# Moving the keys and values of a memory from behind the experts into an earlier mixer, and gathering expert rows without scale and bias

## The chip, the cores and the metric

One core of one Trainium2 chip runs the whole program in one launch. The metric is the device time of one execution in microseconds (us), lower is better; several executions give a median. TensorE (PE) multiplies matrices, VectorE (DVE) and ScalarE (ACT) work element by element, GpSimd (POOL) and SyncE (SP) here mostly issue DMA transfers. Weights lie in HBM and are brought to SBUF by DMA; matmuls accumulate in PSUM.

## The reference, cut to what matters

Two transformer blocks follow one another on 256 tokens of 1024 channels, all in float32.

```python
for l in range(2):                                   # first block
    mix = hybrid_mixer(x, ...)                       # delta rule, convolution branch, forgetting attention
    x = layer_norm(ALPHA * x + mix, ln_mix_g[l], ln_mix_b[l])
    ff = swiglu(x, ...) if l == 0 else moe_swiglu(x, ...)     # top 2 of 8 experts of width 3584
    x = layer_norm(ALPHA * x + ff, ln_ffn_g[l], ln_ffn_b[l])
# second block
x = x + 0.5 * swiglu_ffn(rms_norm(x, ffn1_norm), ...)
mem_kv = rms_norm(mem, mem_norm) @ w_mem_kv          # memory: 256 tokens, depends on inputs alone
m_k, m_v = split(mem_kv); m_k = rms_norm(m_k per head, m_k_gain)
...                                                  # second mixer: attention, state space, memory attention
x = x + 0.5 * swiglu_ffn(rms_norm(x, ffn2_norm), ...)
return rms_norm(x, final_norm)
```

The memory's keys and values need nothing of the first block; they are read only in the second block's mixer.

## The kernel before, in words

**Arithmetic.** A float32 product is made of three matmuls in a faster format: each operand is split into a high and a low part (hi x hi, hi x lo, lo x hi; `mm3`, L183 to L185). A weight tile is loaded by SP (`load`, L166) into one of a ring of places, 1 MB each, and `part` splits each half of it: ScalarE copies it to `wh` (L172), VectorE subtracts to get `wl` (L174). `proj_a` and `proj_b` are projections of 48 matmuls each (256 columns) into a PSUM bank with the tag `a`.

**Order.** The stages stand one behind the other in `build`: mixer 0, ffn0, mixer 1, MoE, ffn1, mixer 2, ffn2, final norm. Within a stage the code emits pieces, and the framework's list scheduler sets the order on each engine's queue; what is emitted earlier has precedence. `issue_after` holds operations of one engine behind a named one. The places of the load ring are a list (`self.places`): 4 `raw` tiles normally; in the MoE also `early0` to `early4`, the tile `rows`, and the two operands `xTh` and `xTl`.

**Mixer 1** emits the delta rule's inverse, its scan, the forgetting attention, the convolution branch (which holds one of the two PSUM banks `a` from its first matmul until L765) and last the gates (L787: one `proj_b` of 48 matmuls, a copy L790, a sigmoid, a product L792). Behind these the parts of the mixed output are transposed and split, the convolution's part last (L802, L803), and the output projection runs.

**MoE.** `layer_norm_T` normalises the rows (L852), transposes them, applies scale and bias on the transposed copy (L859, L860), and then also applies scale and bias to the rows themselves: four operations of 128x1024 on VectorE (L867). The router's logits (L907), the choice of two experts, and the position of each token in its expert's list (`pos`, L921 to L925) follow. The rows are split to `xtokh` and `xtokl` (L930, L931). `gather` brings the rows of an expert into 128 slots by matmuls with a 0/1 matrix (L994), 8 matmuls a step and 4 steps an expert; the high part goes to `xeh` (L996, ScalarE), the low part to `xel` (L998, VectorE). Four experts have 128 slots, and the other four stand in two pairs with 64 each, whose high and low gathers are added into one `xef` (L1000). The loop then runs 42 steps of up projection, activation and down projection; `combine` adds weighted results to the accumulator `acc` (L1062 to L1070), which starts as ALPHA times the rows (L1113, one operation).

**End of the MoE.** Before the last combine, `memory_load` fetches the memory's normalised transposed rows (`memd`, written to DRAM in ffn0) and the weights `mem_k` and `mem_v`, and splits three of their four halves. The statistics of the next layer norm (L1146) and seven small operations that count tokens beyond an expert's slots (L1150 to L1156) follow. An `If` (L1159) holds a path for such tokens, which is not taken here. Behind it come the layer norm (L873 to L879), `rms_T` (squares L1234, scaling L1239, transposes L267), `memory_keys` (2 x 48 matmuls, a head norm with L1263, L1265 and L1267, a copy, a store) and then ffn1.

Of the kernel before, what the change touches and what calls it, by code (L numbers as in the profile page):

```python
# [28 lines left out]
NE = 8  # L29
# [74 lines left out]
class Net:  # L104
# [249 lines left out]
    def mixer1(self, l, x, xT):  # L354
# [443 lines left out]
        self.emit(inverse(), scan(), fox(), conv(), gates())  # L798
# [43 lines left out]
    def layer_norm_T(self, tp, tag, r, st, rows, name, n=4, z_="lnz", bufs=4):  # L842
# [58 lines left out]
    def moe(self, fp, x, xT):  # L901
# [23 lines left out]
        V.tensor_scalar(pos, pos, -1.0, None, op0=ALU.add)  # L925

# [50 lines left out]
        def gather(u, g):  # L977
# [11 lines left out]
            for k in range(0, 8, 2):  # L989
                pg = self.ps("t", "gat").rearrange("p (a k n) -> p a k n", a=2, k=2)  # L990
                for j in range(2):
                    for a, src in enumerate((xh, xl)):
                        for t in range(2):
                            PE.matmul(pg[:, a, j, :], src[:, t, (k + j) * P:(k + j) * P + P], o[:, t],  # L994
                                      start=t + a + j == 0, stop=t == 1, skip_group_check=True)
                S.activation(g[0][:, k:k + 2, :], pg[:, 0], AF.Copy)  # L996
                if len(u) == 1:
                    self.last = V.tensor_copy(g[1][:, k:k + 2, :], pg[:, 1])  # L998
                else:
                    self.last = V.tensor_tensor(g[0][:, k:k + 2, :], g[0][:, k:k + 2, :], pg[:, 1], op=ALU.add)  # L1000
                if k == 6 and u != (0,):
                    back[u] = places(u)
                yield
# [54 lines left out]
        def combine(py, ohT, gp):  # L1058
# [5 lines left out]
            for t in range(2):  # L1064
                for h in range(2):
# [4 lines left out]
                    V.tensor_tensor(acc[:, t, hs], acc[:, t, hs], pc, op=ALU.add)  # L1070

# [40 lines left out]
        with self.tc.issue_after(self.last.ins):  # L1112
            V.tensor_scalar(acc, x, ALPHA, None, op0=ALU.mult)  # L1113
# [27 lines left out]
        st = self.new_stats()  # L1141

        def stats():
            for t in range(2):
                for h in range(2):
                    V.bn_stats(out=st[:, t, h, :], in_=acc[:, t, h * 512:h * 512 + 512])  # L1146


        cap, mxf, mxi = fp.tile([P, NE], F32, name="cap"), fp.tile([P, 1], F32, name="mxf"), fp.tile([P, 1], I32, name="mxi")
        V.tensor_scalar(cap, rank, 3.5, 64.0, op0=ALU.is_lt, op1=ALU.mult)  # L1150
        V.tensor_scalar(cap, cap, 64.0, None, op0=ALU.add)
        V.tensor_tensor(pos, pos, cap[:, None, :].to_broadcast([P, 2, NE]), op=ALU.subtract)
        V.tensor_tensor(cap, cnt, cap, op=ALU.subtract)
        V.tensor_reduce(mxf, cap, axis=AX.X, op=ALU.max)
        V.tensor_scalar(mxf, mxf, 0.0, None, op0=ALU.max)
        V.tensor_copy(mxi, mxf)  # L1156
        most = nc.values_load(mxi[0:1, 0:1], min_val=0, max_val=T)
        stats()
        with self.tc.If(most > 0):  # L1159
            ecur = fp.tile([P, 1], F32, name="ecur")  # L1160
            V.memset(ecur, 0.0)
            with self.tc.For_i(0, NE, 1) as e:
# [18 lines left out]
                for k in range(8):  # L1181
# [4 lines left out]
                    V.tensor_copy(x2[:, k, :], pg[:, :P])  # L1186
# [37 lines left out]
                stats()  # L1224
        return acc, st, mem
# [31 lines left out]
    def norm_heads(self, tp, ps, n, gain, out, tag="g", sq="nhsq"):  # L1257
# [4 lines left out]
        sq = tp.tile([P, 512], F32, name=sq, bufs=2)  # L1262
# [69 lines left out]
    def memory_load(self, fp, tags):  # L1332

        mT = [fp.tile([P, 8, T], F32R, name="memT", tag=t) for t in tags]
        for i in range(2):
            self.nc.gpsimd.dma_start(mT[i], self.memd[i])
        raw = [self.load(self.A[n]) for n in ("mem_k", "mem_v")]
        return mT, raw, [self.part(raw[0]), self.part(raw[0], 1024), self.part(raw[1])]

    def memory_keys(self, fp, mT, raw, parts):  # L1340

        kept = self.keep_mem(fp, tag="y")
        ps = self.proj_a(None, mT, parts=parts[:2])
        self.table(SILU, self.norm_heads(fp, ps, 2, self.col2("mkg"), self.mkT.rearrange("p c t -> p (c t)"), "y", "mos"))
        ps = self.proj_b(None, mT, parts=[parts[2], self.part(raw[1], 1024)])
        self.nc.scalar.activation(self.mv, ps, AF.Copy)
        self.memk = self.dp.tile([P, 1024], F32, name="memk")
        self.nc.gpsimd.dma_start(self.memk, kept)
# [499 lines left out]
def build(tc, A, out):  # L1848
    with ExitStack() as ctx:
# [18 lines left out]
        with net.banks(a=2, y=4, t=2), pool("moe") as fp:  # L1868
            rows = net.load_rows(fp.tile([P, 2, D], F32, name="rows"), "ln_mix", 2, 2)
            xT = net.layer_norm_T(fp, "t", r, st, rows, "mix1", z_="mos", bufs=2)  # L1870
            r, st, mem = net.moe(fp, r, xT)
# [3 lines left out]
            net.memory_keys(fp, *mem)  # L1875
# [28 lines left out]
```

## Time and profile before

| | us |
|---|---|
| median of 3 runs | 2171.85 |
| lowest and highest | 2169.86, 2173.09 |
| profiled execution | 2181.34 |
| its span in the trace | 2179.6 |
| TensorE busy in it | 2085.4 |
| VectorE busy | 1301.9 |
| ScalarE busy | 1021.4 |

The durations in the trace belong to the profiled execution, and sums are made against its time. The span runs from the first to the last instruction; the rest of the execution's time lies around it. A busy TensorE is not a TensorE at its peak: the clock that it was granted is given apart, as a share of full speed (1.00 is 2.4 GHz, 0.50 is 1.2 GHz).

### The profile page before, as it was taken

The page shows a single profiled execution, that of the slowest core. Times are in us where ns is not written, and L with a number is a line of the kernel's source. Part 1 is how long each engine was busy: PE and PEld are TensorE (multiplying, and loading weights), DVE is VectorE, ACT ScalarE, POOL GpSimd, SP SyncE. Part 2 cuts the span into 40 slices and gives each one's busy share as a digit, 9 for nine tenths or more (in the row PEclk, how much of TensorE's full clock was granted, in tenths as well). Part 3 has the DMA queues.
Part 4 walks back from the last instruction along what each step waited for, and adds up shares of the span by engine and source line. Part 5 has one row for each costly group of instructions (what it writes and reads, how often), then busy time and mean ns, then how long its engine had stood idle before and what let it go on. Part 6 is the DMA issues. An engine that isn't in the chain of part 4 may idle for free. (4 is left out here: it accounts for less than half of the span.)

```text
span 2179.6 us, 31865 instructions
## 1 busy us (share of the span) xinstructions
PE 2085.4 (96%) x12770; PEld 1606.4 (74%) x12770; DVE 1301.9 (60%) x1911; ACT 1021.4 (47%) x1453; POOL 13.0 (1%) x27
## 2 busy tenths in 40 slices
PE   8998999899979999999999999999799999999998
PEld 7887999788766565566565566554799988888997
DVE  6767954766676555555465455443655568665544
ACT  6545444464545444444354345442544444544443
POOL 0000000000000000000000000000000000000000
PEclk9979999998979999999999999999899999999999
DMA  6313675322359999999999999998455553444552
GB/s 236 103 44 117 213 261 179 136 88 98 140 181 348 363 407 381 412 419 376 404 367 396 387 404 406 417 415 352 171 188 191 187 176 125 136 164 155 184 183 97
DMA packets 78987, 545.37 MB, mean 250 GB/s; under 512 B 8960, under 2 KB 11272, under 8 KB 13936
## 3 DMA queue, kind: packets, MB, share of 16 engines
q1 hardware_dynamic: 76112, 527.40, 63.4%
q0 software_dynamic: 2720, 15.86, 2.0%
q8 instruction: 103, 1.69, 0.3%
q14 instruction: 52, 0.43, 0.1%
HBM read 536.74 MB, written 6.49 MB: 249 GB/s over the span
## 5 line engine op out<-in xcount | busy, mean ns | idle before, releaser
L174 DVE TENSOR_TENSOR wl<-raw,wh 128x1024 fp32r<-128x1024 f32 (+1 forms) x662 | 798.1, 1217 | 436.4 <-ACT wh L172 422.4
L172 ACT ACTIVATE wh<-raw 128x1024 fp32r<-128x1024 f32 (+1 forms) x662 | 690.6, 1054 | 629.0 <-PE a_pA L184 276.1
L183 PE MATMUL a_pA<-xTh,wh 128*128 128x256 f32 x1456 | 421.0, 290 | 5.9 <-ACT foxqk L620 3.3
L185 PE MATMUL a_pA<-xTh,wl 128*128 128x256 f32 x1456 | 417.9, 287 | 0.9 <-DVE wl L174 0.9
L184 PE MATMUL a_pA<-xTl,wh 128*128 128x256 f32 x1456 | 418.2, 287 | 0.0
L183 PEld LDWEIGHTS a_pA<-xTh,wh 128*128 128x128 f32 x1456 | 283.4, 195 | 13.7 <-ACT foxqk L620 5.3
L184 PEld LDWEIGHTS a_pA<-xTl,wh 128*128 128x128 f32 x1456 | 283.5, 195 | 4.8 <-issue 3.4
L185 PEld LDWEIGHTS a_pA<-xTh,wl 128*128 128x128 f32 x1456 | 283.3, 195 | 4.2 <-issue 2.7
L1021 PE MATMUL a_up<-raw,xef 128*64 128x512 f32 x896 | 213.5, 596 | 0.0
L184 PE MATMUL a_up<-wl,xeh 128*128 128x512 f32 x448 | 180.7, 403 | 0.5 <-DVE wl L174 0.4
L183 PE MATMUL a_up<-wh,xeh 128*128 128x512 f32 x448 | 177.3, 399 | 0.0
L185 PE MATMUL a_up<-wh,xel 128*128 128x512 f32 x448 | 177.1, 395 | 0.0
L1021 PEld LDWEIGHTS a_up<-raw,xef 128*64 128x64 f32 x896 | 65.2, 137 | 127.7 <-issue 122.6
L183 PE MATMUL a_pB<-wh,xTh 128*128 128x256 f32 x480 | 142.0, 297 | 5.0 <-ACT glu L620 3.1
L1026 DVE TENSOR_TENSOR mos<-mos,a_up 128x512 f32<-128x512 f32 x42 | 28.7, 684 | 192.2 <-PE a_up L1021 141.5
L184 PE MATMUL a_pB<-wl,xTh 128*128 128x256 f32 x480 | 140.4, 293 | 0.0
L185 PE MATMUL a_pB<-wh,xTl 128*128 128x256 f32 x480 | 139.4, 293 | 0.6 <-DVE xTl L278 0.6
L1054 PE MATMUL y_y<-raw,mof 128*64 128x512 f32 x448 | 132.8, 602 | 0.7 <-ACT mof L1040 0.7
L184 PEld LDWEIGHTS a_up<-wl,xeh 128*128 128x128 f32 x448 | 84.6, 189 | 35.1 <-issue 12.2
L183 PEld LDWEIGHTS a_up<-wh,xeh 128*128 128x128 f32 x448 | 84.6, 189 | 27.5 <-ACT wh L172 7.3
L185 PE MATMUL acc_acc<-wh,ffl 128*128 128x512 f32 x264 | 102.0, 392 | 0.0
L184 PE MATMUL acc_acc<-wl,ffh 128*128 128x512 f32 x264 | 101.9, 392 | 0.0
(558 smaller groups left out, 2717.9 us busy)
## 6 DMA issues: line engine op xcount, KB each, us to landing
raw<-in_moe_w_dram SPq DMA_DIRECT2D x336, 1024.0 KB, 9.3
raw<-in_ffn_in_dram SPq DMA_DIRECT2D x44, 1024.0 KB, 4.8
raw<-in_ffn_w_dram SPq DMA_DIRECT2D x33, 1024.0 KB, 4.9
raw<-in_w_in_a_dram SPq DMA_DIRECT2D x24, 1024.0 KB, 5.0
raw<-in_ffn_out_dram SPq DMA_DIRECT2D x22, 1024.0 KB, 4.8
raw<-in_w_out_dram SPq DMA_DIRECT2D x12, 1024.0 KB, 4.9
raw<-in_w_in_g_dram SPq DMA_DIRECT2D x12, 1024.0 KB, 4.9
raw<-in_w_in_b_dram SPq DMA_DIRECT2D x6, 1024.0 KB, 5.0
```

What stands on the lines that cost most here:

```text
L172: nc.scalar.activation(wh[:, :m], raw[:, o:o + m], AF.Copy)
L174: nc.vector.tensor_tensor(wl[:, :m], raw[:, o:o + m], wh[:, :m].bitcast(F32), op=ALU.subtract)
L183: mm(out, lh, rh, start=start, stop=False, skip_group_check=True)
L184: mm(out, lh, rl, start=False, stop=False, skip_group_check=True)
L185: mm(out, ll, rh, start=False, stop=stop, skip_group_check=True)
L1021: PE.matmul(ps[r], xe[0][:, k0, r], w[:, k * 512:k * 512 + 512], start=k0 == 0, stop=k0 == 7, skip_group_check=True)
L1026: V.tensor_tensor(s, s, pp[1], op=ALU.mult)
L1054: PE.matmul(py[h][r], hf[:, k, r], w[:, j * 1024 + h * 512:j * 1024 + h * 512 + 512], start=b == 0 and k == 0, stop=b == 6 and k == 3, ski ...
```

## The change

1. Memory's keys and values are computed in mixer 1, emitted between the convolution branch and the gates. The transposed rows of the memory come by two POOL loads into two of the four `raw` tiles; the weights come through the ordinary load ring. Keys and values are stored in two halves from tiles with the tag `sg`. `memory_load` and the call behind `rms_T` go.
2. In the MoE `layer_norm_T` no longer applies scale and bias to the rows. The gather sums the high and low gathers in one PSUM region; two ScalarE activations of 128x128 per step then apply scale and bias (a scalar per partition, from `gain` and `shift`). For a 128-slot expert another copy and a subtraction split the result again. The accumulator is made by four operations of 128x1024 that apply ALPHA, scale and bias, and that read `rows`. The path under the `If` applies scale and bias as well.
3. The count of tokens beyond the slots is emitted at step 4 of the loop instead of behind it; its value is still read at the end.
4. The statistics are emitted one by one behind each of the last adds.

```diff
@@ mixer1
-        self.emit(inverse(), scan(), fox(), conv(), gates())
+        self.emit(inverse(), scan(), fox(), conv(), *([self.memory_keys(mp)] if l else []), gates())
@@ layer_norm_T
-        with self.tc.issue_after(last.ins):
-            for t in range(2):
-                for i, op in enumerate((ALU.mult, ALU.add)):
-                    V.tensor_tensor(r[:, t, :], r[:, t, :], rows[:, i], op=op)
+        if rows is not None:
...
@@ moe, gather
-                pg = self.ps("t", "gat").rearrange("p (a k n) -> p a k n", a=2, k=2)
+                pg = self.ps("t", "gat")[:, :T].rearrange("p (k n) -> p k n", k=2)
                 for j in range(2):
                     for a, src in enumerate((xh, xl)):
                         for t in range(2):
-                            PE.matmul(pg[:, a, j, :], src[:, t, (k + j) * P:(k + j) * P + P], o[:, t],
-                                      start=t + a + j == 0, stop=t == 1, skip_group_check=True)
-                S.activation(g[0][:, k:k + 2, :], pg[:, 0], AF.Copy)
+                            PE.matmul(pg[:, j, :], src[:, t, (k + j) * P:(k + j) * P + P], o[:, t],
+                                      start=t + a + j == 0, stop=a + t == 2, skip_group_check=True)
+                z = fp.tile([P, 2, P], F32, name="gz", bufs=2) if len(u) == 1 else g[0][:, k:k + 2, :]
+                for j in range(2):
+                    last = S.activation(z[:, j, :], pg[:, j, :], AF.Identity, scale=gain[:, k + j:k + j + 1], bias=shift[:, k + j:k + j + 1])
                 if len(u) == 1:
-                    self.last = V.tensor_copy(g[1][:, k:k + 2, :], pg[:, 1])
-                else:
-                    self.last = V.tensor_tensor(g[0][:, k:k + 2, :], g[0][:, k:k + 2, :], pg[:, 1], op=ALU.add)
+                    S.activation(g[0][:, k:k + 2, :], z, AF.Copy)
+                    self.last = V.tensor_tensor(g[1][:, k:k + 2, :], z, g[0][:, k:k + 2, :].bitcast(F32), op=ALU.subtract)
@@ moe, accumulator, count, last combine
         with self.tc.issue_after(self.last.ins):
-            V.tensor_scalar(acc, x, ALPHA, None, op0=ALU.mult)
+            for t in range(2):
+                V.scalar_tensor_tensor(acc[:, t, :], x[:, t, :], ALPHA, rows[:, 0], op0=ALU.mult, op1=ALU.mult)
+                V.scalar_tensor_tensor(acc[:, t, :], rows[:, 1], ALPHA, acc[:, t, :], op0=ALU.mult, op1=ALU.add)
...
+            if n == 4:
+                overflow()
...
-        self.places = [(fp, "early2"), (fp, "early3")]
-        mem = self.memory_load(fp, ("early0", "early1"))
         self.places = [(self.raw, "raw")] * 4
-        combine(py[prev[0]], *back[prev[0]])
...
+        combine(py[prev[0]], *back[prev[0]], last=True)
@@ memory_keys
+    def memory_keys(self, mp):
+
+        mT = [self.raw.tile([P, 8, T], F32R, name="memT", tag="raw", bufs=4) for _ in range(2)]
+        for t, src in zip(mT, self.memd):
+            self.nc.gpsimd.dma_start(t, src)
         self.memk = self.dp.tile([P, 1024], F32, name="memk")
+        kT, v = (mp.tile([P, 2, T], F32, name="sg", bufs=3) for _ in range(2))
+        self.norm_heads(mp, self.proj_a(self.A["mem_k"], mT), 2, self.col2("mkg"), kT.rearrange("p c t -> p (c t)"), sq="sg", bufs=3)
+        self.nc.gpsimd.dma_start(self.memk[:, :512], kT.rearrange("p c t -> p (c t)"))
+        self.nc.scalar.activation(v, self.proj_b(self.A["mem_v"], mT), AF.Copy)
+        self.nc.gpsimd.dma_start(self.memk[:, 512:], v.rearrange("p c t -> p (c t)"))
+        yield
@@ build
-            xT = net.layer_norm_T(fp, "t", r, st, rows, "mix1", z_="mos", bufs=2)
-            r, st, mem = net.moe(fp, r, xT)
+            xT = net.layer_norm_T(fp, "t", r, st, None, "mix1", z_="mos", bufs=2)
+            r, st = net.moe(fp, r, xT, rows)
...
-            net.memory_keys(fp, *mem)
```

## Rows read from the trace of the kernel before

**Rows 1.** The page, section 1: busy us, share of the span, instructions.

```profile
PE 2085.4 (96%) x12770; PEld 1606.4 (74%) x12770; DVE 1301.9 (60%) x1911; ACT 1021.4 (47%) x1453; POOL 13.0 (1%) x27
```

**Rows 2.** Windows: stretch, its length, busy PE, PEld, DVE, ACT, POOL, clock, DMA share, GB/s.

```profile
530.00:550.00 20.00, 20.00 (x155) 13.44 (x153) 9.40 (x29) 6.78 (x26) 0.00 (x0) 0.50 0.00 1
...
555.00:576.00 21.00, 21.00 (x186) 18.35 (x184) 16.36 (x36) 10.32 (x19) 0.00 (x0) 1.00 0.01 4
576.00:581.00 5.00, 2.40 (x14) 1.57 (x12) 3.76 (x10) 4.29 (x12) 0.00 (x0) 1.00 0.15 20
581.00:587.00 6.00, 4.78 (x22) 4.09 (x22) 3.97 (x10) 3.58 (x7) 0.53 (x1) 0.72 0.91 371
```

**Rows 3.** Windows of the MoE's start and of its loop, same columns.

```profile
610.00:640.00 30.00, 19.11 (x84) 15.93 (x85) 24.57 (x72) 13.39 (x22) 0.00 (x0) 0.56 0.40 141
...
700.00:1500.00 800.00, 792.37 (x3384) 467.12 (x3384) 421.56 (x413) 360.27 (x403) 0.00 (x0) 1.00 0.98 397
```

**Rows 4.** Timeline at the MoE's end, and line L1159's branch (nanoseconds: min/median/max).

```profile
1536.49 1.21 DVE L174 TENSOR_TENSOR wl<-raw,wh 128x1024 fp32r<-128x1024 f32 x1
...
1537.86 0.55 PE L183 MATMUL a_pA<-memT,wh 128*128 128x256 f32 x1 [6.34 <-DVEq L1159]
...
L1159 PEldq COMPARE_BRANCH  x1: 3737/3737/3737, 1531.4 to 1531.4; - x1
```

**Rows 5.** Timeline from the If to ffn1's first matmul.

```profile
1540.48 2.48 DVE L879 SCALAR_TENSOR_TENSOR x<-x,bnrs,rows 128x1024 f32<-128x1024 f32 x2
...
1543.76 1.05 ACT L1234 ACTIVATE rmsx<-x 128x1024 f32<-128x1024 f32 x1
...
1549.62 1.02 PE L1265 MATMUL y_nh<-mos,call 128*128 128x512 f32 x2
...
1559.30 0.56 PE L183 MATMUL a_pA<-xTh,wh 128*128 128x256 f32 x1
```

**Rows 6.** Timeline ahead of ffn2: the same norm without memory.

```profile
1974.96 1.04 ACT L1234 ACTIVATE rmsx<-x 128x1024 f32<-128x1024 f32 x1
...
1982.21 0.52 PE L183 MATMUL a_pA<-xTh,wh 128*128 128x256 f32 x1 [0.20 <-DVE xTl L278]
```

**Rows 7.** Tile memT: ns min/median/max, first and last start in us.

```profile
L183 PE MATMUL a_pA<-memT,wh x16: 276/276/550, 1537.9 to 1545.1; 128*128 128x256 f32 x16
...
L183 PE MATMUL a_pB<-wh,memT x16: 276/276/280, 1545.4 to 1551.4; 128*128 128x256 f32 x16
```

**Rows 8.** Timeline of mixer 1: gates' matmuls, convolution bank, output projection.

```profile
534.44 0.56 PE L183 MATMUL a_pB<-wh,xTh 128*128 128x256 f32 x1
...
567.32 0.28 PE L184 MATMUL a_pB<-wl,xTh 128*128 128x256 f32 x1
...
572.79 0.69 DVE L765 TENSOR_TENSOR ccv<-ccv,a_conv 128x512 f32<-128x512 f32 x1 [0.58 <-PE a_conv L362]
...
587.28 0.39 PE L183 MATMUL a_pB<-wh,xTh 128*128 128x256 f32 x1 [0.65 <-ACT xTh L802]
```

**Rows 9.** Timeline at the MoE's start.

```profile
620.04 3.49 DVE L867 TENSOR_TENSOR x<-x,rows 128x1024 f32<-128x1024 f32 x3
...
625.72 0.16 DVE L907 COPY lg<-t_pSt 128x16 f32<-128x16 f32 x1
625.80 1.21 DVE L931 TENSOR_TENSOR xtokl<-x,xtokh 128x1024 fp32r<-128x1024 f32 x1
...
629.35 0.57 PE L922 MATMUL t_pos<-sel,call 128*128 128x8 f32 x2 [6.00 <-DVE g L1104]
...
642.49 1.22 DVE L1113 TENSOR_SCALAR x<-x 128x2048 f32<-128x2048 f32 x1
```

**Rows 10.** Lines by form: busy us, mean ns; idle before and its releasers.

```profile
L458 ACT ACTIVATE E<-g_dec,cum 128x128 f32<-128x128 f32 x24 | 7.3, 363 | 3.3 <-PE g_dec L362 3.3
L998 DVE CAST xel<-t_gat 128x256 fp32r<-128x256 f32 x16 | 6.7, 421 | 6.6 <-ACT xeh L996 6.5
L996 ACT ACTIVATE xeh<-t_gat 128x256 fp32r<-128x256 f32 x16 | 6.2, 385 | 12.9 <-PE t_gat L994 12.9
```

More of the change, by code (lines that the diff above doesn't have):

```diff
@@ L863, in layer_norm_T @@
             last = V.tensor_tensor(lo[:, k:k + 2, :], z, hi[:, k:k + 2, :].bitcast(F32), op=ALU.subtract)
-        with self.tc.issue_after(last.ins):
-            for t in range(2):
-                for i, op in enumerate((ALU.mult, ALU.add)):
-                    V.tensor_tensor(r[:, t, :], r[:, t, :], rows[:, i], op=op)
+        if rows is not None:
+            with self.tc.issue_after(last.ins):
+                for t in range(2):
+                    for i, op in enumerate((ALU.mult, ALU.add)):
+                        V.tensor_tensor(r[:, t, :], r[:, t, :], rows[:, i], op=op)
         return xT
@@ L897, in residual_ffn1, with moe @@
         return r, st
-    def moe(self, fp, x, xT):
+    def moe(self, fp, x, xT, rows):
         nc, A, ident = self.nc, self.A, self.ident
@@ L925, in moe @@
         V.tensor_scalar(pos, pos, -1.0, None, op0=ALU.add)
+        gain, shift = self.col1("mix1g"), self.col1("mix1b")
         xh, xl = fp.tile([P, 2, D], F32R, name="xtokh"), fp.tile([P, 2, D], F32R, name="xtokl")
@@ L1056, in down, with stats, combine @@
                     k += 1
-        def combine(py, ohT, gp):
+        st = self.new_stats()
+        def stats(t, h):
+            V.bn_stats(out=st[:, t, h, :], in_=acc[:, t, h * 512:h * 512 + 512])
+        def combine(py, ohT, gp, last=False):
             yh, yl = fp.tile([P, 2, D], F32R, name="y").rearrange("p a n -> a p n")
@@ L1070, in combine @@
                     V.tensor_tensor(acc[:, t, hs], acc[:, t, hs], pc, op=ALU.add)
+                    if last:
+                        stats(t, h)
         def places(u):
@@ L1112, in moe, with overflow @@
         with self.tc.issue_after(self.last.ins):
-            V.tensor_scalar(acc, x, ALPHA, None, op0=ALU.mult)
+            for t in range(2):
+                V.scalar_tensor_tensor(acc[:, t, :], x[:, t, :], ALPHA, rows[:, 0], op0=ALU.mult, op1=ALU.mult)
+                V.scalar_tensor_tensor(acc[:, t, :], rows[:, 1], ALPHA, acc[:, t, :], op0=ALU.mult, op1=ALU.add)
+        cap, mxf, mxi = fp.tile([P, NE], F32, name="cap"), fp.tile([P, 1], F32, name="mxf"), fp.tile([P, 1], I32, name="mxi")
+        def overflow():
+            V.tensor_scalar(cap, rank, 3.5, 64.0, op0=ALU.is_lt, op1=ALU.mult)
+            V.tensor_scalar(cap, cap, 64.0, None, op0=ALU.add)
+            V.tensor_tensor(pos, pos, cap[:, None, :].to_broadcast([P, 2, NE]), op=ALU.subtract)
+            V.tensor_tensor(cap, cnt, cap, op=ALU.subtract)
+            V.tensor_reduce(mxf, cap, axis=AX.X, op=ALU.max)
+            V.tensor_scalar(mxf, mxf, 0.0, None, op0=ALU.max)
+            V.tensor_copy(mxi, mxf)
         prev, py, steps = None, {}, iter(())
@@ L1223, in moe @@
                         V.tensor_tensor(acc[:, t, hs], acc[:, t, hs], py, op=ALU.add)
-                stats()
-        return acc, st, mem
+                for i in range(4):
+                    stats(i // 2, i % 2)
+        return acc, st
     def rms_T(self, ps, tp, x, gains, silu=False, **kw):
@@ L1255, in ffn2, with norm_heads @@
         return r
-    def norm_heads(self, tp, ps, n, gain, out, tag="g", sq="nhsq"):
+    def norm_heads(self, tp, ps, n, gain, out, tag="g", sq="nhsq", bufs=2):
         nc = self.nc
@@ L1261, in norm_heads @@
         pv = ps.rearrange("p c t -> p (c t)")
-        sq = tp.tile([P, 512], F32, name=sq, bufs=2)
+        sq = tp.tile([P, 512], F32, name=sq, bufs=bufs)
         nc.scalar.activation(sq[:, :w], pv, AF.Square)
@@ L1330, in keep_mem @@
         return t
[L1332 to L1346, printed above, removed]
-        self.memk = self.dp.tile([P, 1024], F32, name="memk")
-        self.nc.gpsimd.dma_start(self.memk, kept)
+    def memory_keys(self, mp):
+        mT = [self.raw.tile([P, 8, T], F32R, name="memT", tag="raw", bufs=4) for _ in range(2)]
+        for t, src in zip(mT, self.memd):
+            self.nc.gpsimd.dma_start(t, src)
+        self.memk = self.dp.tile([P, 1024], F32, name="memk")
+        kT, v = (mp.tile([P, 2, T], F32, name="sg", bufs=3) for _ in range(2))
[4 more added lines that the diff above has]
+        yield
     def prepare2(self, tp):
```

16 lines of the change are left out of this document (1 added, 15 removed).

## The prediction, made before the changed kernel was run

> **What bounds the kernel now.** I read the page's busy shares first, then the windows by stage, and only then single waits. TensorE is busy for 96% of the span [rows 1], so the only time to be had is where it idles or runs at half clock. The windows show three such places near this change. From 576 to 587 us, between the scan of the first block's second mixer and its output projection, TensorE works 2.40 of 5 us and then 4.78 of 6: 3.8 us idle [rows 2]. From 610 to 640 it works 19.11 of 30 us at a granted clock of 0.56 [rows 3]. Behind the experts it stands still for 6.34 us before the first memory matmul, released by VectorE's sequencer at the If [rows 4]. The stretch between, 700 to 1500 us, has TensorE at 792.37 of 800 us and the DMA engines at a share of 0.98 [rows 3]: there a few more instructions on ScalarE or VectorE cost only what they delay TensorE by.
>
> The row of 530 to 550 us matters as well: 20.00 of 20 us busy, no idle at all, but a granted clock of 0.50, which is 1.2 GHz; from 555 it is 1.00 [rows 2].
>
> **Part 1: memory leaves the end of the MoE.** Two things go. First, three splits `wl` of 1.2 us each ran on VectorE among the last adds and statistics; the last one starts at 1536.49 and ends at 1537.70, and TensorE is released at 1537.86 [rows 4]. Without them VectorE is through at about 1537.7 - 3.6 = 1534.1. Then TensorE's own branch is late next: it starts at 1531.4 and takes 3737 ns, to 1535.1 [rows 4]. So the barrier comes at about 1535.3, 2.4 us earlier; the bounds are 0 (another engine is as late) and 2.5.
>
> Second, the 96 memory matmuls stand ahead of the transposes on TensorE's queue, and ffn1's first matmul runs at 1559.30, 21.4 us after the release [rows 5]. Without memory the chain is layer norm, squares, transposes. The layer norm's last operation starts at 1540.48 and takes 2.48 us, so it ends 5.1 us after the release [rows 5]. From there the same code stands undisturbed ahead of ffn2: squares from 1974.96, first matmul at 1982.21, so 7.25 us [rows 6]. Together 12.4 us; I take 13 for the gap of 0.8 us that also stands between L879's end and the squares now [rows 5]. That is 8.4 us saved. The table load, copies and splits of memory that sat on ScalarE in between go too, and so are in this difference; the SILU table is now loaded by ffn1 itself, on ScalarE ahead of its first evacuation, beside the matmuls that are to be evacuated; without that cover it costs one table load. The sum is 10.8 us; I take **-10**, since neither end has shown itself alone, with bounds of -7 and -11.5.
>
> **Part 2: memory arrives in the mixer.** The 96 matmuls cost here what they cost at the end: the second projection's first matmuls start at 1545.4 and its last at 1551.4 [rows 7]. With its 0.3 us tail it took 6.3 us, the head norm's pair (1.02 us [rows 5]) in it; twice that less one pair is 11.6 us at full clock. At half clock the 96 alone take nearly twice as long, 20 us, which is the upper bound (the first projection, from 1537.9 to 1545.1, is the longer one because it began so [rows 7]). None of it finds idle time before 576, because TensorE is back to back; only the 3.8 us between 576 and 587 can take some [rows 2]. So 11.6 - 3.8 = 7.8: I take **+8**, with 16 as the upper bound (20 less 3.8). The lower bound is about -1, by the rival on the clock below.
>
> The order matters too. Memory is emitted ahead of the gates' projection, the filler of today, which runs in pieces from 534.44 to 567.32 [rows 8]. The new matmuls take these places and the gates' go behind. The convolution holds one of the two `a` banks until 572.79 [rows 8], so two memory projections and the gates' share the other. The two loads on SP's queue, the two on POOL's and the two stores cost nothing: the DMA share is 0.00 and 0.01 there [rows 2]. They take the four raw slots ahead of the output projection's weights, whose loads move behind; those have the empty DMA stretch until 582 to land. If that cover were gone, one load's landing would be paid once. ScalarE's and VectorE's pieces (four splits, the head norm) are moved, not added, and fall where both are about half idle.
>
> **Part 3: no scale and bias on the rows.** The four L867 operations, three of them in 3.49 us from 620.04, held VectorE with one split until 625.7, when the router's logits were copied [rows 9]. Two 1.2 us subtractions for the row splits followed them, and the positions' matmul waited 6.00 us until 629.35 [rows 9]. Without L867 the copy can go at about 623.5 and the subtractions ahead of it, so up to 4.6 us are saved; some of it is lost to splits that move up, and an earlier start counts only as far as loads and TensorE can use it: **-3**, bounds 0 and -5.
>
> The accumulator was one operation of 1.22 us at 642.49 [rows 9]; now it is four, each like half of L879's pair, 1.24 us [rows 5]: 3.7 us more on VectorE just when the first splits are wanted, so 0 to +3.7. The `rows` tile is one of the places of the load ring and is now released only behind them, some 18 us later; the load that takes it, and those behind it on SP's queue, wait. The share of DMA in 610 to 640 is 0.40, with stock in the other places, so I price that within the same **+2**, with 5 as the upper bound.
>
> Gathers: a single expert's step had a 0.385 us copy on ScalarE and 0.421 on VectorE [rows 10]. The nearest row for an activation of 128x128 with pointer operands out of PSUM is 0.363 [rows 10]. So ScalarE has 2 x 0.363 + 0.385 = 1.11, 0.73 more in each of 16 steps, 11.6 us in all; VectorE stays. A pair's step has 0.73 for the same 0.385 copy on ScalarE and loses an addition on VectorE, in 8 steps. Spread over a loop whose TensorE is 99% busy most is hidden, but the first expert's four steps lie on the path to the first up projection: **+1.5**, bounds 0 and +5. The same count of gather matmuls remains. The overflow count's seven small operations move but ran early already: 0. Inline statistics are the same four operations: 0.
>
> **Sum**: -10 + 8 - 3 + 2 + 1.5 = -1.5 us. The profiled execution took 2181.34 us (span 2179.6), so it would take 2179.8. It lies 9.5 above the median of the runs, 2171.85, to which I apply the same difference: **2170.4**.
>
> **Rivals.** *The clock holds* (0.32). In 530 to 550 TensorE is never idle and yet at half clock; what runs there are narrow matmuls and, from 534.44, the gates' pieces. The row from 555 on, in which the gates' pieces end, has 1.00 [rows 2, 8]. If memory's 128x128 blocks keep it at 2.4 GHz through those 20 us, the same work takes 10, and most of the 8 us come back: mixer about 0, total -9.5, 2162.3. Against it: the gates' first matmul, at 534.44, took 0.56 us where the last took 0.28, and the clock stayed low [rows 8]. The Trainium skill (TensorE: Matmul & The Clock Gate, What's actually happening) says that throttled is the default state and that activity releases it. By that rule the time would come out as in this rival; the trace agrees only as far as the clock rose where wide matmuls stood denser.
>
> *The gates end last* (0.20), the other side. Two memory projections on one bank, at half clock, push the gates' projection behind the scan; its copy, sigmoid, product and transposes then stand ahead of the output projection, which now restarts at 587.28 on the convolution's branch [rows 8]. Price: the upper bound of +16 in the mixer, total +6.5, 2178.4. It decides if the gates' last matmul, now at 567.32, comes after about 577.
>
> *The loop pays* (0.08): accumulator, released place and longer gather steps each at their upper bounds, 5 + 5, with none of the 3 us of the early router kept: total +8, 2179.9. Against it, TensorE's 99%.
>
> That memory isn't in the mixer's pieces but is scheduled behind its scan is the second rival's mechanism at a lower price.
>
> **How the numbers follow.** The forecast has 0.40, the rivals 0.32, 0.20 and 0.08. 0.2% is 4.3 us, about what a measurement of this kernel can tell from no change. The forecast's own bounds (2165 to 2176) lie mostly within that, so a fifth of it goes to faster and a tenth to slower. Faster: 0.32 less a little, plus 0.08, 0.38. Slower: most of 0.28, 0.24. Same: 0.38. The range goes from a little under the clock case, 2160, to just above the gates' case, 2179; the forecast's own range is 2165 to 2176.
>
> **What the profile of after would show.** Right: memory's matmuls between 515 and 580 us with output projection starting 5 to 10 us later; first ffn1 matmul about 13 us behind the If's release; `t_pos` some 4 us earlier after the layer norm's statistics; 530 to 550 still near 0.5. Wrong: a granted clock near 1 in that stretch; gate copies behind the scan; or a TensorE idle group in the loop released by ScalarE's gather copies.

## The result, and the profile after

| | before | after |
|---|---|---|
| median, us (6 runs each, taken side by side) | 2172.73 | 2187.57 |
| lowest and highest | 2169.86, 2179.87 | 2182.94, 2197.01 |
| ratio, 95% interval | | 1.0076 [1.006, 1.0092] |
| profiled execution, its span | 2181.34, 2179.6 | 2186.54, 2184.8 |

The change makes the kernel 0.76% slower, about 16.5 us (13 to 20). Forecast was no change, 2170.4, with 2179 as the top of the range: sign and range are both wrong. The two profiled executions are only 5 us apart; before's was a long one, and its stage of the first block's second mixer was long as well (below).

The busy totals of after, from the page, answer to [rows 1]: TensorE does the same 12770 matmuls in 8.5 us less busy time and a span longer by 5.2 us, so the loss is idle time.

```profile
PE 2076.9 (95%) x12770; PEld 1594.8 (73%) x12770; DVE 1299.8 (59%) x1902; ACT 1036.6 (47%) x1493; POOL 13.4 (1%) x28
```

Windows of after, the stretches and columns of [rows 2, 3]:

```profile
530.00:550.00 20.00, 20.00 (x210) 15.60 (x211) 14.31 (x42) 9.76 (x31) 0.00 (x0) 0.82 0.01 2
555.00:576.00 21.00, 21.00 (x181) 18.34 (x180) 11.51 (x25) 9.23 (x17) 0.55 (x1) 1.00 0.19 64
576.00:581.00 5.00, 5.00 (x44) 5.00 (x44) 2.76 (x4) 4.16 (x6) 0.55 (x1) 1.00 0.87 332
581.00:587.00 6.00, 1.17 (x11) 0.93 (x9) 3.79 (x7) 5.42 (x10) 0.00 (x0) 0.83 0.98 398
610.00:640.00 30.00, 19.68 (x126) 16.63 (x124) 21.21 (x61) 12.14 (x21) 0.00 (x0) 0.82 0.50 176
700.00:1500.00 800.00, 787.83 (x3348) 463.88 (x3345) 422.98 (x410) 372.12 (x433) 0.00 (x0) 1.00 0.97 393
```

Three things stand out. From 530 to 550 the granted clock is 0.82 where it was 0.50, so more was done there (210 matmuls, not 155). From 576 to 581 TensorE is now full, but from 581 to 587 it works 1.17 of 6 us. In the loop it lost 4.54 us of 800 (792.37 to 787.83).

**Mixer.** The timeline of after shows where the new hole comes from; it answers to [rows 8].

```profile
531.79 0.56 PE L183 MATMUL a_pA<-memT,wh 128*128 128x256 f32 x1
...
575.59 0.28 PE L183 MATMUL a_pB<-wh,xTh 128*128 128x256 f32 x1
...
581.23 0.28 PE L185 MATMUL a_pB<-wh,xTl 128*128 128x256 f32 x1
...
581.55 0.60 ACT L790 ACTIVATE gate<-a_pB 128x512 f32<-128x512 f32 x1 [1.30 <-PE a_pB L185]
...
587.44 0.96 DVE L792 TENSOR_TENSOR gate<-gate,late 128x768 f32<-128x768 f32 x1 [1.12 <-ACT late L301]
...
591.09 1.02 DVE L816 TENSOR_TENSOR mixed<-late,mixed 128x384 f32<-128x384 f32 x2
...
591.70 1.59 PE L267 MATMUL g_tr<-call,mixed 128*128 128x128 f32 x6 [9.53 <-DVE mixed L816]
593.63 0.58 PE L183 MATMUL a_pB<-wh,xTh 128*128 128x256 f32 x1 [0.35 <-ACT xTh L277]
```

Memory's matmuls stand among the scan's from 531.79 on, and the gates' 48 run only from 575.59 to 581.23. Their copy (L790), product (L792) and the mixed parts behind them (L816) have nothing beside them: TensorE waits 9.53 us.

**End of the MoE.** Timeline of after, answering to [rows 4, 5]; the first row is L1169's branch, the If of after (nanoseconds).

```profile
L1169 PEldq COMPARE_BRANCH  x1: 3706/3706/3706, 1546.4 to 1546.4; - x1
...
1549.44 0.20 ACT L874 ACTIVATE bnrs<-bnst 128x2 f32<-128x2 f32 x1 [5.76 <-DVEq L1169]
...
1553.51 1.06 ACT L1245 ACTIVATE rmsx<-x 128x1024 f32<-128x1024 f32 x1 [2.02 <-DVE x L880]
...
1555.36 2.00 ACT L172 ACTIVATE wh<-raw 128x1024 fp32r<-128x1024 f32 x2 [0.69 <-DMA raw<-in_ffn_in_dram]
...
1557.26 1.04 ACT L1245 ACTIVATE rmsx<-x 128x1024 f32<-128x1024 f32 x1
...
1558.47 1.06 ACT L172 ACTIVATE wh<-raw 128x1024 fp32r<-128x1024 f32 x1
...
1559.44 0.28 ACT L293 ACTIVATE rmss<-rmss,bias 128x2 f32<-128x2 f32 x1
...
1561.60 2.11 PE L267 MATMUL t_tr<-call,rmsx 128*128 128x128 f32 x8 [15.06 <-DVE rmsx L1250]
...
1566.87 0.56 PE L183 MATMUL a_pA<-xTh,wh 128*128 128x256 f32 x1
```

Three splits of ffn1's weights (L172, some 3 us) stand in ScalarE's queue between the two squares (L1245) and ahead of the norm's logarithm (L293). The chain that was to run undisturbed is held up by them, and TensorE sits idle for 15.06 us.

**The stages.** Worked out from first and last starts in each trace: *mixer* from the norm behind ffn0 (L852) to the norm at the MoE's start (L852 again); *router* from there to `t_pos`; *gather* to the first up projection; *loop* to the end of the last `y_y`; *tail* to the first operation behind the If; *norm* to ffn1's first matmul on `xTh`. In us:

| run | mixer | router | gather | loop | tail | norm |
|---|---|---|---|---|---|---|
| before | 201.4 | 18.5 | 5.8 | 892.8 | 9.9 | 21.5 |
| after | 212.5 | 14.4 | 7.2 | 899.8 | 6.5 | 17.4 |
| e1 memory only | 215.2 | 17.0 | 5.8 | 895.6 | 6.5 | 17.6 |
| e3 gates before memory | 208.3 | 14.4 | 7.2 | 898.0 | 6.5 | 17.4 |
| e4 squares first | 215.2 | 14.4 | 7.1 | 900.0 | 6.5 | 15.0 |
| e7 move well placed | 205.4 | 17.0 | 5.8 | 895.3 | 6.5 | 14.9 |
| e8 end reordered | 196.5 | 18.5 | 5.8 | 892.6 | 6.5 | 19.1 |
| e2 rows only | 196.3 | 16.2 | 7.1 | 898.8 | 9.9 | 20.7 |
| e10 count and statistics | 201.7 | 18.5 | 5.8 | 896.4 | 9.9 | 21.7 |
| e11 shift only | 193.2 | 18.5 | 5.8 | 896.5 | 9.9 | 21.6 |
| e12 rows replaced | 201.5 | 16.2 | 7.3 | 894.9 | 9.8 | 22.4 |
| e13 end and places | 197.8 | 18.5 | 5.8 | 890.2 | 6.5 | 19.7 |
| e14 after replaced | 212.5 | 14.4 | 7.2 | 894.9 | 6.5 | 17.8 |

The same mixer code took 193.2 to 201.7 us in the ten profiles that have it as before (mean 198.6, e5, e6 and e9 among them), so one profile can't price a mixer to better than a few us. The four with memory ahead of the gates took 212.5 to 215.2 (mean 213.9).

### The profile page after: what moved, and what is told of

It is laid out like the page before. It is cut to its first block, busy times and chain, and to the rows that moved or that the text cites. A ratio compares the mean times of both kernels' runs of the same rounds, so it can differ in the third digit from the quotient of the medians.

```text
span 2184.8 us, 31901 instructions
## 1 busy us (share of the span) xinstructions
PE 2076.9 (95%) x12770; PEld 1594.8 (73%) x12770; DVE 1299.8 (59%) x1902; ACT 1036.6 (47%) x1493; POOL 13.4 (1%) x28
## 5 line engine op out<-in xcount | busy, mean ns | idle before, releaser
L174 DVE TENSOR_TENSOR wl<-raw,wh 128x1024 fp32r<-128x1024 f32 (+1 forms) x662 | 798.6, 1218 | 400.1 <-ACT wh L172 394.9
L172 ACT ACTIVATE wh<-raw 128x1024 fp32r<-128x1024 f32 (+1 forms) x662 | 690.5, 1053 | 598.5 <-PE a_pA L184 271.7
L183 PE MATMUL a_pA<-xTh,wh 128*128 128x256 f32 x1456 | 420.0, 289 | 5.9 <-ACT foxqk L620 3.3
L183 PEld LDWEIGHTS a_pA<-xTh,wh 128*128 128x128 f32 x1456 | 281.7, 194 | 13.6 <-ACT foxqk L620 5.3
L183 PE MATMUL a_up<-wh,xeh 128*128 128x512 f32 x448 | 178.4, 401 | 0.0
L183 PE MATMUL a_pB<-wh,xTh 128*128 128x256 f32 x480 | 140.1, 293 | 4.0 <-ACT glu L620 3.1
L183 PEld LDWEIGHTS a_up<-wh,xeh 128*128 128x128 f32 x448 | 84.5, 189 | 27.6 <-ACT wh L172 6.7
```

The costliest lines, as they stand in the source:

```text
L172: nc.scalar.activation(wh[:, :m], raw[:, o:o + m], AF.Copy)
L174: nc.vector.tensor_tensor(wl[:, :m], raw[:, o:o + m], wh[:, :m].bitcast(F32), op=ALU.subtract)
L183: mm(out, lh, rh, start=start, stop=False, skip_group_check=True)
```

## The experiments

### The change in two halves

e1 is the kernel before with part 1 of the change alone; e2 is the changed kernel with memory put back at the end.

```diff
# e1: before, with
+        self.emit(inverse(), scan(), fox(), conv(), *([self.memory_keys(mp)] if l else []), gates())
# e2: after, with
-        self.emit(inverse(), scan(), fox(), conv(), *([self.memory_keys(mp)] if l else []), gates())
+        self.emit(inverse(), scan(), fox(), conv(), gates())
```

> The kernel before with memory's keys and values moved into the first block's second mixer and nothing else of the change. Theory A (the loss is the move: the gates' projection ends behind memory's, and the output projection waits for them): layer norm behind the mixer about 10 us later than before, memory's place at the end gives back about 8, so 2 us slower than before if the expert loop is untouched by the move. Theory B (the loss is the expert loop, through the gather's extra ScalarE work and the four accumulator operations): this kernel, which has none of these, shows a loop as long as before, 892 us from the first up projection to the last down projection in the trace, and is at most 4 us from before. Theory C (the later, differently stocked start of the weight stream makes the loop longer, whatever the gather does): loop about 7 us longer here too, and the kernel 8 to 12 us slower than before.

> The changed kernel with memory's keys and values back behind the experts: rows without scale and bias, early count and inline statistics remain. Theory A: the router's positions 3 to 4 us earlier than before, loop unchanged, so 2 to 4 us faster than before. Theory B: the loop is 7 to 14 us longer than before and the kernel 4 to 11 us slower than before. Theory C: like A.

Measured: e1 1.0039 [1.0024, 1.0055], e2 1.0015 [0.9999, 1.0031]. The move loses about 8.5 us (5 to 12), where the sum's half had -2. The rows with count and statistics come out about 3 us slower, but that interval reaches no change, so the +0.5 of the sum's other half is not excluded. No single theory fits: e1 is as slow as theory C said, with a loop only 2.8 us longer than before's; e2's loop is 6.0 us longer, a little under theory B's 7 to 14, and its time is below B's 4 us.

### What the move costs where

```diff
# e3: after, with
-        self.emit(inverse(), scan(), fox(), conv(), *([self.memory_keys(mp)] if l else []), gates())
+        self.emit(inverse(), scan(), fox(), conv(), gates(), *([self.memory_keys(mp)] if l else []))
# e4: after, with rms_last the last operation of the norm's reciprocal root in rms_T
-        self.ffn(fp, lambda j: w[j], lambda j: w[11 + j], lambda j: o[j], xT, evac)
+        with self.tc.issue_after(self.rms_last.ins):
+            self.ffn(fp, lambda j: w[j], lambda j: w[11 + j], lambda j: o[j], xT, evac)
# e7: e1 with both edits
```

> The changed kernel with the gates emitted ahead of memory, so that memory's matmuls are the last filler. Theory A: the wait of 9.5 us for the mixed output shrinks to 2 us or less, the output projection starts 6 to 9 us earlier than in the changed kernel, and the whole is 6 to 9 us faster than that one. Rival: TensorE is simply full in the mixer, the 96 matmuls cost their 11 us whatever stands last, and the kernel is within 3 us of the changed one.

> The changed kernel with ScalarE's work of both later feed-forward stages queued behind the reciprocal root of their norm. In the changed kernel ScalarE's second square, at the end of the MoE, stands behind two weight splits that wait for their load, and the root behind a third. Theory A: the first matmul of ffn1 comes about 13 us behind the If's release instead of 17.5, and the kernel is 3 to 4.5 us faster than the changed one. Rival: the splits, now later, hold the first matmuls instead, since the loads are only issued at the If; then less than 1.5 us is won.

> Memory's move alone, with the gates emitted ahead of it and ScalarE's work of the later feed-forward stages behind the root of their norm. Theory A (the move cost 8 us because the gates ended last): mixer 7 to 9 us shorter than in e1, 15.0 us from the If's release to ffn1's first matmul, so 0 to 2 us from before. Rival (the 96 matmuls have no idle time to lie in): still 4 us or more slower than before.

e3 1.0038 [1.0023, 1.0054], against after's 1.0076: about half of the loss was the order of gates and memory. Its longest wait of TensorE from 560 to 610 us is 1.4 us, where after's is 9.5; some 2.4 us of the second window stay idle:

```profile
530.00:550.00 20.00, 20.00 (x168) 15.13 (x168) 11.49 (x33) 9.60 (x28) 0.00 (x0) 0.68 0.00 1
...
576.00:587.00 11.00, 8.61 (x58) 7.17 (x57) 9.01 (x17) 9.22 (x20) 1.64 (x3) 1.00 0.71 251
```

e4 1.0076 [1.0054, 1.0097]: the squares do come first, and the norm takes 15.0 us instead of 17.4 (13 was expected), but no time is gained that the runs can show. e7 1.0029 [1.0012, 1.0045]: with both orders repaired the move alone still costs about 6 us. Its mixer is 205.4 us against a mean of 198.6, and its end is worth 10 (tail -3.4, norm -6.6); with router -1.5 and loop +2.5 the profiles put the move at -2, and the runs, which are more, at a loss of 6; where the difference lies was not found. The move gains nothing even in the better order.

### Was the end's time memory's, or its order's?

e8 is the kernel before with memory left where it was: its splits stand ahead of the last combine on ScalarE and VectorE, and the rest of its head norm behind ffn1's operands, with the second projection emitted ahead of it.

```diff
-        combine(py[prev[0]], *back[prev[0]])
+        with self.tc.issue_after(self.pa.ins), self.tc.issue_after(self.pv.ins):
+            combine(py[prev[0]], *back[prev[0]])
...
+        pb = self.proj_b(None, mT, parts=[parts[2], self.part(raw[1], 1024)])
+        after = (self.sT, self.sV)
+        self.table(SILU, self.norm_heads(fp, ps, 2, self.col2("mkg"), self.mkT.rearrange("p c t -> p (c t)"), "y", "mos", after))
+        with self.tc.issue_after(self.sT.ins):
+            self.nc.scalar.activation(self.mv, pb, AF.Copy)
```

> The kernel before with memory left where it was, in another order: the last combine's ScalarE and VectorE work behind memory's first three splits (both engines are idle for 6 to 8 us before it), and memory's head norm and copy behind the operands of ffn1. Theory A (most of what the move saved at the end was order, not matmuls): release at the If 6.5 us after the last down projection instead of 9.9, ffn1's first matmul 16.5 to 18 us behind it instead of 21, so 5 to 7 us faster than before. Rival: memory's 96 matmuls themselves hold the transposes, and less than 4 us is won.

Measured 2165.26, ratio 0.9962 [0.9945, 0.9978]: faster than both kernels, by some 8 us where 5 to 7 were expected. Its timeline at the end:

```profile
1526.20 0.55 PE L183 MATMUL a_pA<-memT,wh 128*128 128x256 f32 x1 [3.95 <-PEq L1160]
...
1544.29 0.38 PE L183 MATMUL a_pA<-xTh,wh 128*128 128x256 f32 x1 [2.55 <-ACT mos L293]
```

The tail is 6.5 us, as in after, and the first memory matmul waits 3.95 us for TensorE's own branch (PEq), not 6.34 for VectorE. The tail's saving is thus had without moving anything, and the 18 us to ffn1's first matmul hold memory's 96 matmuls, where after has 15 us of idle TensorE. Memory stood in time that the norm leaves mostly empty: with it the norm takes 19.1 us, without it 17.4 (after) or 15.0 (e4).

### Which operation makes the loop longer?

e5 and e6 undo one part of e2 each and leave work out: e5 gathers as before, so the experts' rows lack scale and bias; e6 starts the accumulator with one operation, so that it lacks them. e9 is the kernel before without L867, so that both lack them. e10 is the kernel before with parts 3 and 4 of the change alone.

```diff
# e6: e2, with
-            for t in range(2):
-                V.scalar_tensor_tensor(acc[:, t, :], x[:, t, :], ALPHA, rows[:, 0], op0=ALU.mult, op1=ALU.mult)
-                V.scalar_tensor_tensor(acc[:, t, :], rows[:, 1], ALPHA, acc[:, t, :], op0=ALU.mult, op1=ALU.add)
+            V.tensor_scalar(acc, x, ALPHA, None, op0=ALU.mult)
# e9: before, with
-            xT = net.layer_norm_T(fp, "t", r, st, rows, "mix1", z_="mos", bufs=2)
+            xT = net.layer_norm_T(fp, "t", r, st, None, "mix1", z_="mos", bufs=2)
# e10: before, with
+            if n == 4:
+                overflow()
...
+        combine(py[prev[0]], *back[prev[0]], last=True)
```

> The rows part alone (memory at the end, as in e2), but with the gather of before: the experts get rows without scale and bias. Read by the loop, first up projection to last down projection, which was 892.8 us before, 895.6 with memory moved alone, and 898.0 to 900.0 in four kernels with the rows part. Theory G (the gather's two extra ScalarE operations a step make the loop longer): 893 to 896 here. Theory K (the accumulator's four operations and the later release of their place in the load ring do): 898 to 900 here.

> The rows part alone, but the accumulator starts from ALPHA times the rows in one operation, without scale and bias, and the rows tile is free at once. Theory G: loop 898 to 900 us. Theory K: loop 893 to 896 us, and the kernel about 5 us faster than the rows part alone.

> The kernel before without the four L867 operations and nothing in their place: the rows that the experts gather and the accumulator starts from have no scale and bias. Gather, accumulator, count, statistics and memory as before. Open is why the loop is 898 to 900 us long in every kernel with the rows part, also with the old gather (900.1) or the old accumulator (898.3). Theory E (the earlier start of the gather, with the queue orders that come of it, is not kept: the weight stream gives it back over the loop): 898 to 900 here too, and the time from the layer norm to the last down projection about 4 us more than before's 917. Theory O (the early count or the inline statistics cost it): loop 893 to 896 and the time from the layer norm to its end 3 us less than before's.

> The kernel before with the early count of tokens beyond the slots and the statistics behind each last add, and nothing else of the change. Theory O: loop 898 to 900 us and the kernel 4 to 6 us slower than before. Theory E: loop 893 to 896, and the kernel within 2 us of before.

Measured: e5 1.002 [1.0001, 1.0039], e6 0.9998 [0.998, 1.0016], e9 0.9971 [0.9953, 0.9989], e10 1.0039 [1.0022, 1.0057]. The loops of e5 and e6 are 900.1 and 898.3 us, as long as e2's 898.8: neither gather nor accumulator alone is the cause, and e6's ratio, 0.17% under e2's, is within the two intervals. e9 shows that dropping L867 is a gain by itself; its loop is 894.5 us. The surprise is e10, which I had priced at nothing: 0.39% slower, with a loop of 896.4 us between what the two theories gave. TensorE's waits in its loop are those of before to the tenth (5.3, 2.7 and 0.4 us), and yet the loop is 3.6 us longer. What it has besides is 96 bytes of small tiles that are allocated ahead of later ones, so that those lie elsewhere in SBUF.

### The place in SBUF

e11 and e12 widen one small tile by columns that nothing reads; e13 and e14 widen two. Every engine's instructions keep their order. A place is given as its remainder within 1024 bytes of a partition, as the program lays its tiles out; the traces don't show it.

```diff
# e11: before, 24 floats; e12: e2, 232; e13: e8, 32; e14: after, 32
-        ids, idi, w2 = fp.tile([P, NE], F32, name="ids"), fp.tile([P, NE], I32, name="idi"), ...
+        ids, idi, w2 = fp.tile([P, NE + 24], F32, name="ids")[:, :NE], fp.tile([P, NE], I32, name="idi"), ...
# e13: 224 more floats behind the first pair of operands; e14: 200
-        g = fp.tile([P, 4, 2], F32, name="g")
+        g = fp.tile([P, 8 + 224], F32, name="g")[:, :8].rearrange("p (a t) -> p a t", a=4)
```

> The kernel before with one small tile of the first stage's constants made 24 floats wider than it needs (96 bytes of each partition); every engine has the same instructions in the same order, and only the places in SBUF of the tiles that are allocated behind it move by 96 bytes, as they do with the early count. Theory P (the place in SBUF of the experts' operands sets how fast their matmuls follow one another): the experts' loop takes 896 to 897 us and not 893, the mean of L183's matmuls from 700 to 1500 us goes from 157.7 to about 158.5 ns, and the whole is 0.15 to 0.4% slower, by the early count's 1.0039 and its loop's 3.6 us. Theory N (the place does not matter, and the early count lost its time by its own instructions): the loop stays at 893 us, L183 at 157.7 ns, ratio 1.000.

> The kernel with the rows without scale and bias, the early count and the memory's projections at the end, with the same tile made 232 floats wider (928 bytes), so that the pair of expert operands that was slow gets back the place, counted within 1024 bytes, that it has in the kernel before; the order of every engine's instructions is unchanged. Theory P, if it is the place within 1024 bytes that counts: the loop goes from 898.8 back to 893 to 896 us and the whole to a ratio of 0.998 to 0.9995 to the kernel before, where the same kernel without the shift had 1.0015. Theory N (the rows part costs the loop its time by its instructions): loop 898 to 900 us, ratio 1.001 to 1.002. If the place counts but not by the remainder within 1024 bytes, the loop stays at 898 to 900 as well, and only the run with the 96 bytes tells.

> The kernel with the end of the experts' stage reordered (no other part of the change), with two small tiles made wider (128 and 896 bytes) so that both pairs of single experts' operands lie at the same place within 1024 bytes, 224, where so far only the second pair did; the tiles that the loads land in keep their remainder, and the order of every engine's instructions is unchanged. Theory P1 (the place of the operands themselves counts): the first and the third expert's matmuls follow each other as fast as the second's and the fourth's, the loop goes from 892.6 to 887.5 to 890 us, and the ratio from 0.9962 to 0.993 to 0.9955. Theory P2 (the place of the loads' tiles counts, or something else of the placement): the loop stays at 892 to 893.5 us and the ratio at 0.995 to 0.9975.

> The changed kernel with two small tiles made wider (128 and 800 bytes), so that both pairs of single experts' operands and the tiles that the loads land in lie at the remainder of 224 within 1024 bytes; the order of every engine's instructions is that of the changed kernel. Theory P (the changed kernel's longer loop is the place of its operands): its loop goes from 899.8 us to 890 to 895, and its ratio to the kernel before from 1.0076 to 1.003 to 1.0055. Theory N (the longer loop comes from the new gather's instructions): loop 898 to 900 us, ratio 1.006 to 1.009.

Measured: e11 1.003 [1.0011, 1.0049], e12 1.001 [0.9994, 1.0027], e13 0.9952 [0.9932, 0.9972], e14 1.0032 [1.0013, 1.0051]. The rows are those of the lines by form, L183's up projections, 880 to 1000 us (the second expert, second pair of operands) and then 1120 to 1260 (the third expert, first pair). Before:

```profile
L183 PE MATMUL a_up<-wh,xeh 128*128 128x512 f32 x61 | 24.0, 394 | 0.0
...
L183 PE MATMUL a_up<-wh,xeh 128*128 128x512 f32 x76 | 30.3, 399 | 0.0
```

e11, 96 bytes on:

```profile
L183 PE MATMUL a_up<-wh,xeh 128*128 128x512 f32 x64 | 25.5, 399 | 0.0
...
L183 PE MATMUL a_up<-wh,xeh 128*128 128x512 f32 x74 | 29.5, 399 | 0.0
```

e12, where the second pair has its old place within 1024 bytes again:

```profile
L183 PE MATMUL a_up<-wh,xeh 128*128 128x512 f32 x64 | 25.2, 394 | 0.0
...
L183 PE MATMUL a_up<-wh,xeh 128*128 128x512 f32 x78 | 31.1, 399 | 0.0
```

e13, where the first pair has that place too:

```profile
L183 PE MATMUL a_up<-wh,xeh 128*128 128x512 f32 x64 | 25.2, 394 | 0.0
...
L183 PE MATMUL a_up<-wh,xeh 128*128 128x512 f32 x75 | 29.8, 397 | 0.0
```

Each pair follows its own place: 394 ns at the remainder of 224 (the second pair in before, e12 and e13), 399 at 96 (before's first pair), 192 and 320 (e11's two) and 0 (e12's first). e13's first pair, moved to 224, has 397 in its row. From one start to the next, within an expert's steps, the difference is clearer: 229.3 ns on the mean for the second expert and 233.1 for the third in before, 233.2 and 233.4 in e11, 229.3 and 229.4 in e13. e13's tiles for the loads keep their remainder while its first pair moved, so it is the place of the experts' operands. Its waits in the loop are those of before, and its loop is 890.2 us against e8's 892.6: 2.4 us for one pair.

The 3.6 us of e10 and e11 hold more than a pair. The operands of the down projections lie behind the second pair and moved with it from 224 to 320, and their matmuls got slower as well. Lines by form of the whole span, before:

```profile
L183 PE MATMUL y_y<-wh,moh 128*128 128x512 f32 x224 | 73.1, 401 | 0.0
```

And e11:

```profile
L183 PE MATMUL y_y<-wh,moh 128*128 128x512 f32 x224 | 73.8, 404 | 0.0
```

In e13, where these operands stayed, it is 401 again. e14 has both pairs and the down operands at 224; it gets 4.9 us of the changed kernel's loop back, and its ratio falls from 1.0076 to 1.0032. Theory P fits e11 and e14, P1 e13 but for 0.2 us in the loop; in e12 the loop came back as expected (894.9), but the ratio lies above the expected 0.998 to 0.9995 and, with an interval of 0.17% to each side, can't be told from e2's 1.0015. Why 224 is fast and the four other remainders aren't, these runs don't say; others weren't tried.

The other part of the loop's loss is waits. TensorE's waits in the loop of before (us, times, longest):

```profile
PE t_hT L1032 <- DVE mos L1026: 5.3, 7, 0.9
PE y_y L184 <- DVE wl L174: 2.7, 2, 1.4
...
PE a_up L184 <- DVE wl L174: 0.4, 1, 0.4
```

And of after:

```profile
PE t_hT L1037 <- DVE mos L1031: 7.8, 10, 0.9
PE a_up L184 <- DVE wl L174: 2.8, 3, 1.6
PE y_y L184 <- DVE wl L174: 2.7, 2, 1.4
```

The sums are 8.4 and 13.3: 4.9 us more, all behind VectorE. Half of it goes with the order of VectorE's queue: e1, with no new operation in the loop, has 7.9 for L1032 and 12.3 in all, and its VectorE runs before's 481 operations with a few in other places, while e10, in before's order, has 8.4. No run changed the order alone. The other half is new work, for `a_up` waits 2.4 us more, most of it at one point:

```profile
656.18 0.50 PE L184 MATMUL a_up<-wl,xeh 128*128 128x512 f32 x1 [1.64 <-DVE wl L174]
```

From 648.77 to 654.99 VectorE runs the accumulator's four operations (L1126, L1127), and the splits that TensorE needs stand behind them. In e2 this wait is 1.64 us too; in e6, with the accumulator of before, it is gone. That e6's loop is all the same only 0.5 us shorter comes later: it is 1.6 us ahead of e2 up to the tenth step, and then, in another order, loses that again.

## Why the prediction was wrong, point by point

- **Mixer, +8 with 16 as the upper bound: the wrong case.** The text saw that memory takes the gates' places and that the gates may then end last, and gave that a chance of 0.20. It is what happened: the gates' last matmul comes at 581.23, past the 577 from which that rival was to decide, and the mixer takes 15.3 us more by the means above, where the rival had +16. The wait of 9.5 us and the gates' 5.6 us behind 575.59 make up 15.1 of it. Well placed (e3, e7, two profiles) it takes 8.3 more, so the +8 was about the right price for an order that the kernel doesn't have. The step that failed is the choice between the two: the emission order gave it away, since memory was emitted ahead of the gates, with two projections of 48 matmuls on the one bank and no idle time before 576.
- **The clock.** The rival that had it hold was half right: 0.82, not 0.50 [rows 2], in 530 to 550. The rule of the Trainium skill named there (TensorE: Matmul & The Clock Gate, What's actually happening) agrees with that. What it is worth, some 6 us of full speed (0.32 of 20), seems to have paid for memory's place among the scan: in the four with memory ahead of the gates the scan's last copy (L735) starts 161.7 to 164.4 us into the mixer, in the ten as before 158.5 to 166.9. But the gates and the wait behind them took more than that, so the other half of the rival, that most of the 8 us come back, fell. Nor did the gates' case need the half clock that its text gave it.
- **End, -10 with -7 as a bound.** The tail gave -3.4 instead of -2.4. TensorE's branch is late next, as said (it starts at 1546.4 and takes 3706 ns, to 1550.1), but it holds TensorE alone: ScalarE starts the norm at 1549.44, as soon as VectorE is through. The norm gave -4.1 (21.5 to 17.4) instead of -8.4. The step that failed is "the same code stands undisturbed ahead of ffn2": there the squares follow each other without a gap, here ffn1's first loads land in the middle of the norm and their splits stand between its squares. e4, with the squares first, gives -6.5 there; in it VectorE's splits (L174, 3.57 us from 1561.83) stand ahead of the operands' low parts (L278, 1565.31) instead. -7.5 in all lies inside the bounds.
- **MoE's start, -3, +2 and +1.5.** The router came 4.1 us earlier (e2: 2.3), the gather 1.4 later. The activation of 128x128 took 453 ns, not the 363 of the nearest row, as this row of after's lines by form shows, and the gather stage still cost what was said, by luck as far as that price goes. The accumulator's +2 falls into the loop; the 1.64 us there are close to it. The row:

```profile
L1002 ACT ACTIVATE gz<-t_gat,p 128x128 f32<-128x128 f32 x32 | 12.9, 453 | 15.1 <-PE t_gat L998 14.6 <-DVE xel L1005 0.5
```

- **Loop, "most is hidden".** It is 7.0 us longer. ScalarE's gather copies do not show among TensorE's waits; of the named rival, that the loop pays for accumulator, place in the ring and gather steps, the accumulator's 1.64 us are true. The step that failed is that the loop had no term of its own: missing were a new order on VectorE and the operands' place in SBUF. TensorE's idle time between the first up projection and the last down projection went from 10.5 us to 15.3 (4.8). Of the 4.9 that e14 gives back by place, 2.4 (e8 to e13) lie badly in before too, which leaves 2.5. Together 7.3.
- **Count and statistics, 0 each.** Together +0.39% in e10; the bytes alone, in e11, have +0.30%, so it is the tiles' place.
- **The sum.** 15.3 - 7.5 - 4.1 + 1.4 + 7.0 = +12.1, where -1.5 was forecast; measured are 13 to 20. About 4 us stay unexplained by the stages, and single profiles can't settle that. e10, e11 and e14 also moved the median by some 3 to 5 us more than their loop.

## What to carry to other kernels

Work that is moved into a stretch with little idle TensorE time costs most of its length there (8.3 of 11.6 us here, in the better order), and if it is emitted ahead of the stretch's filler, the filler goes to the end and its epilogue with it: look first for what else could run in the place that the work leaves. Here memory's 96 matmuls stood in time that a norm leaves mostly empty, and reordering around them (e8, 0.9962; with the operands' places, e13, 0.9952) beat both kernels. Before a loss of a few us in a long loop is put down to an edit's instructions, run the kernel before with the same bytes added as columns that nothing reads.

## What the runs showed of the hardware

Within an expert's steps a 128x512 matmul followed the one before after 229.3 or 233.3 ns, by where its 128x128 operand lay in SBUF: a difference of nearly 2% from 96 bytes, with every instruction and every wait of the loop the same, at a granted clock of 1.00. It showed in up and in down projections. For one pair of experts' operands it was 2.4 us of a loop of some 890 (e13 against e8); for a pair and the down operands together 3.6 (e10 and e11 against before). That the matmul and not a transfer is slower is seen from e13; what in the chip does it was not tried.
